# Making the operands of two weight matrices once, beside the attention, and loading their parts later: an encoder layer on one core

## The chip, the core and the metric

The kernel runs on one core of a Trainium2 chip. The metric is the device time of one execution in microseconds (us), the median of several runs. The engines are called PE (TensorE: matmuls, with PEld for its weight loads), DVE (VectorE), ACT (ScalarE), POOL (GpSimd) and SP (SyncE, which here only issues DMAs).

## The reference

One encoder layer in float32 on 2048 tokens of width 1024:

```
proj = x @ w_in                     # queries, keys, values of 16 heads, 8 forget gates
y    = 8 heads of forgetting attention, 8 heads of chunked band attention
x    = layer_norm(alpha * x + concat(y) @ w_out, ln1)       # w_out: 1024 x 1024
u    = causal conv of width 3 over x @ w_up                 # w_up: 1024 x 5632
h    = value * gelu(gate)                                   # halves of u, 2816 wide
out  = layer_norm(alpha * x + h @ w_down, ln2)              # w_down: 2816 x 1024
```

## The kernel before

*Three matmuls for one product.* Each operand of a large product is kept as two float32r parts of 128x512: a high part, a rounded copy that ACT makes (`split`, line 172), and a low part, the source minus the high part, a subtraction on DVE or POOL (line 175). `mm3` (lines 179 to 181) adds up high x high, high x low and low x high in PSUM.

*Seven products for eight.* The up- and down-projections multiply 2 by 2 blocks with seven block products. The table `DOWN` says for each of the seven which block of h, or sum or difference of two, meets which block of w_down, or sum or difference of two, and to which output blocks the product goes. Five of the seven have a sum on the side of h, five on the side of w_down. `combine` makes such an operand: the sum (line 1045), the high part, the low part.

*Stages.* The projection writes queries, keys and values to DRAM, in two halves of 1024 tokens, in steps of three matmuls for each of the 8 slices k of the width; each of the 1024 steps is a `yield`. The attention goes through work items (head pair, head, chunk of 512 tokens). `weave` runs both, a piece of attention and then so many steps of the dense work; where the attention needs heads that are not projected yet, the dense work runs alone (`projected`). The dense work goes on with the output projection of chunks 0 and 1. Then a `Pipeline` runs steps written out in a list: output projection of chunk 2, up-projection of chunks 0 and 1, output projection of chunk 3, down-projection of chunks 0 and 1, up- and down-projection of chunks 2 and 3. A step has `load` (issued up to five steps ahead, as buffers allow), `prepare` (splits and sums, two steps ahead) and `multiply`. Chores (norms, transposes, stores) are taken between steps at a fixed pace. All tiles of 128x512 come from `Slots`, a pool of 54 and later 85 buffers.

*The order within an engine* follows these priorities, as the framework puts the instructions out ahead of time; each engine then works strictly in order. All loads and stores are issued by SP, in one queue.

*Which engine makes a part.* In `out_steps` weights are split by ACT and POOL, tokens by ACT and DVE. In the down-projection h is split by ACT and DVE, w_down by ACT and POOL; sums go to DVE or POOL as `Choice` says, a running account of both engines' work that charges 0.6 for DVE and 1.23 for POOL, lets the account fall by a step's time, and prefers DVE by 3. The down-projection goes through all 11 k of one product before the next (n = 2 and 4 together), in the order 3, 6, 1, 2 and 4, 5, 7, and runs twice, for chunks 0 and 1 and for chunks 2 and 3. So each operand of w_down is made twice, each of w_out four times. One step has 12 matmuls of 512 columns in the down-projection, 24 in the output projection.

Of the kernel before, what the change touches and what calls it, by code (L numbers as in the profile page):

```python
# [19 lines left out]
P = 128  # L20
# [54 lines left out]
    ((3,), ((0, 1), (1, 1)), ((0, 1), (1, 1)), ()),  # L75
    ((6,), ((0, 0),), ((0, 0), (0, 1)), ()),
    ((1,), ((1, 0),), ((0, 0), (1, 1)), ()),
    ((2, 4), (), ((0, 0), (1, 0)), ((1, 0),)),
    ((5,), (), ((1, 1),), ((0, 0),)),
    ((7,), (), ((1, 0), (1, 1)), ((0, 1), (1, 1))),  # L80
)
AHEAD_L, AHEAD_P, RESERVE = 5, 2, 16
# [22 lines left out]
def hymba_layer(  # L105
# [58 lines left out]
    x1t_d = tl(dram, [NCH, KT, P, CH], F32, "x1t_d")  # L164

# [120 lines left out]
    def weave(a, dense, rate):  # L286

        done, start = 0.0, dense.length
        for unit in a:
            done += unit  # L290
            while dense.length - start < done * rate and dense.step():
                pass

# [425 lines left out]
    def out_steps(c, mem, zp, banks, state, done):  # L719
# [4 lines left out]
        def load_tiles(j, ks):  # L724
            for k in ks:
                ws[j, k] = mem.get()
                nc.sync.dma_start(ws[j, k], w_out[k * P : (k + 1) * P, CH * j : CH * j + CH])

        def split_tile(j, k):
            raw = ws[j, k]  # L730
            ws[j, k] = mem.get(F32R), mem.get(F32R)
            split(*ws[j, k], raw, nc.scalar, nc.gpsimd)
            mem.put(raw)

        def product_step(j, t):
# [9 lines left out]
            def prepare():  # L745
                if (j, t) == (0, 0):
                    state["z"] = [{} for _ in range(TQ)]
                    state["stt"] = tl(zp, [P, TQ, 2, 6], F32, "bn", 2)
                    for k, raw in enumerate(ys):
                        split_tile(0, k)  # L750
# [4 lines left out]
            def multiply():  # L755
                acc = banks.get()
                for k in range(KT):
                    mm3(acc, *(y[:, t * P : t * P + P] for y in ys[k]), *ws[j, k], k == 0, k == KT - 1)
                    if t == TQ - 1:
                        mem.put(*ws[j, k])  # L760
                        if j == 0:
                            split_tile(1, k)
# [12 lines left out]
            return Step(load, prepare, multiply, {(0, 0): 32, (0, TQ - 1): WNEXT + 1}.get((j, t), 1), 5.2)  # L775
# [247 lines left out]
    def ffn_down2(ca, mem, zp, banks, gains, later, end):  # L1023
# [63 lines left out]
        def product_step(g, k, n):  # L1087
            ns, blocks, rows, used = DOWN_ORDER[g]
            (i0, j0), u2, aop, (k0, l0), v2, bop, _ = DOWN[n]
            ops = []  # L1090

            def load():
# [5 lines left out]
                if n == ns[0]:  # L1098
                    for i, j in rows:
                        w[g, k, i, j] = mem.get()  # L1100
                        r0 = (HF * i + k) * P
                        nc.sync.dma_start(f32(w[g, k, i, j]), w_down[r0 : r0 + P, CH * j : CH * j + CH])

            def prepare():
                ops.extend(combine(h[i0, j0, k], u2 and h[(*u2, k)], aop, nc.vector))
                ops.extend(combine(w[g, k, k0, l0], v2 and w[(g, k, *v2)], bop, nc.gpsimd))
                if n == ns[-1]:
                    mem.put(*(w.pop((g, k, *b)) for b in rows), *(h.pop((*b, k)) for b in used))
# [34 lines left out]
    with ExitStack() as st:  # L1143
# [42 lines left out]
        def dense_work():  # L1186
            yield from projection(mem, banks, state)
# [26 lines left out]
        with ExitStack() as inner:  # L1214
            projected(1)
# [103 lines left out]
```

## Time and profile before

| | us |
|---|---|
| median of 3 runs | 2919.07 (2910.76 to 2919.12) |
| the profiled execution's own time | 2915.05 |
| its span, from the first to the last instruction | 2913.2 |

| engine | busy us | share of the span | instructions |
|---|---|---|---|
| PE | 2763.0 | 95% | 12632 |
| DVE | 2000.8 | 69% | 3333 |
| ACT | 1247.7 | 43% | 2165 |
| POOL | 1255.8 | 43% | 1178 |

Mean granted clock of TensorE: 0.974 of full speed. DMA moved 399.43 MB, a mean of 137 GB/s.

The table gives means over stages that differ. A busy PE can be a PE that is fed slowly: a stretch is better judged by its number of matmuls than by its busy time. In rows of waits the instruction that waited stands left of the arrow, the one that ended the wait right of it. In rows of groups the line may be that of a helper: line 175 is every low part, whoever asked for it.

### The profile page before, as it was taken

How to read it: one execution, taken by the hardware profiler on the slowest of the kernel's cores; microseconds unless marked ns; L12 is line 12 of the kernel's file. 1: busy time of each engine (PE TensorE's matmuls, PEld its weight loads, DVE VectorE, ACT ScalarE, POOL GpSimd, SP SyncE). 2: the span in 40 equal slices, each digit the busy share in tenths (PEclk: the TensorE clock that was granted, in tenths of full speed). 3: DMA queues.
4: the chain of work that ended last, by engine and by line, in shares of the span. 5: the costliest groups of instructions: out<-in, count | busy, mean ns of one | idle time of the engine just before them, and what ended most of it. 6: DMA issues, size and time to landing. Idle time of an engine off the chain costs nothing.

```text
span 2913.2 us, 38493 instructions
## 1 busy us (share of the span) xinstructions
PE 2763.0 (95%) x12632; PEld 2065.3 (71%) x12632; DVE 2000.8 (69%) x3333; ACT 1247.7 (43%) x2165; POOL 1255.8 (43%) x1178
## 2 busy tenths in 40 slices
PE   8999999999999999998899999998977999999996
PEld 6675767766666667665678888777755888887674
DVE  3446365665454556686877777877798777778878
ACT  3434334344443444444454454533434544454442
POOL 2224331436556654555432211545677211115565
PEclk9999999999999999999999999999988999999998
DMA  6534446443333345646522222577352222228542
GB/s 193 150 120 136 116 154 189 135 139 101 95 106 95 104 139 174 181 154 223 178 84 87 77 83 81 179 239 266 125 166 87 72 84 83 80 76 306 182 141 105
DMA packets 255832, 399.43 MB, mean 137 GB/s; under 512 B 64368, under 2 KB 79856, under 8 KB 255632
## 3 DMA queue, kind: packets, MB, share of 16 engines
q1 hardware_dynamic: 255632, 396.98, 43.1%
q8 instruction: 99, 1.62, 0.2%
q14 instruction: 101, 0.83, 0.1%
HBM read 298.16 MB, written 98.70 MB: 136 GB/s over the span
## 4 chain that ended last, share of the span: by engine, by line
PE 38%; DVE 8%; POOL 3%; DMA 2%; issue 2%; ACT 1%; SPq 0%; POOLq 0%; DVEq 0%; ACTq 0%
PE acc L179 13%; PE acc L180 12%; PE acc L181 12%; DVE slot L175 2%; POOL slot L175 1%; DVE slot L1045 1%; DVE slot L1057 1%; DMA slot<-in_w_down_dram 1%; DVE slot L1075 1%; DVE slot L781 1%; DMA slot<-h_d 1%; ACT slot L172 1%; POOL slot L953 0%; POOL slot L784 0%; DVE slot L870 0%
## 5 line engine op out<-in xcount | busy, mean ns | idle before, releaser
L179 PE MATMUL acc<-slot,slot 128*128 128x512 f32 (+2 forms) x3128 | 1201.7, 384 | 69.0 <-ACT slot L172 31.5
L180 PE MATMUL acc<-slot,slot 128*128 128x512 f32 (+2 forms) x3128 | 1195.0, 382 | 18.6 <-POOL slot L175 18.6
L181 PE MATMUL acc<-slot,slot 128*128 128x512 f32 (+2 forms) x3128 | 1195.0, 382 | 13.9 <-DVE slot L175 12.6
L172 ACT ACTIVATE slot<-slot 128x512 fp32r<-128x512 f32 (+1 forms) x906 | 533.1, 622 | 768.4 <-DVE slot L1045 187.1
L175 POOL TENSOR_TENSOR slot<-slot,slot 128x512 fp32r<-128x512 f32 (+1 forms) x363 | 542.9, 1505 | 512.9 <-ACT slot L172 385.1
L179 PEld LDWEIGHTS acc<-slot,slot 128*128 128x128 f32 x3128 | 602.0, 192 | 196.9 <-ACT slot L172 40.4
L181 PEld LDWEIGHTS acc<-slot,slot 128*128 128x128 f32 x3128 | 600.6, 192 | 138.1 <-DVE slot L175 21.6
L180 PEld LDWEIGHTS acc<-slot,slot 128*128 128x128 f32 x3128 | 602.1, 192 | 135.6 <-POOL slot L175 23.8
L175 DVE TENSOR_TENSOR slot<-slot,slot 128x512 fp32r<-128x512 f32 (+1 forms) x547 | 495.7, 919 | 229.0 <-ACT slot L172 165.7
L598 POOL TENSOR_TENSOR sums<-sums,pt 128x512 f32<-128x512 f32 (+3 forms) x416 | 410.0, 985 | 229.5 <-ACT pt L589 171.3
L589 ACT ACTIVATE pt<-st 128x512 f32<-128x512 f32 (+3 forms) x544 | 262.8, 493 | 390.5 <-PE st L578 140.0
L664 PE MATMUL y<-pt,vv 128*64 128x512 f32 (+3 forms) x1088 | 268.3, 505 | 0.0
L577 PE MATMUL st<-qa,ka 128*128 128x512 f32 (+2 forms) x544 | 210.0, 387 | 8.8 <-ACT pt L589 8.6
L543 DVE TENSOR_REDUCE mx<-sc 128x1 f32<-128x512 f32 x192 | 128.2, 687 | 125.3 <-PE sc L540 123.9
L1045 DVE TENSOR_TENSOR slot<-slot,slot 128x512 f32<-128x512 f32 x180 | 178.6, 1020 | 25.8 <-DMA slot<-in_w_down_dram 9.0
L578 PE MATMUL st<-qb,kb 97*128 97x512 f32 (+2 forms) x544 | 192.0, 359 | 2.8 <-ACT qb L558 2.0
L540 PE MATMUL sc<-kb,qb 66*128 66x512 f32 (+2 forms) x544 | 187.3, 372 | 6.4 <-DMA qb<-qh_d 5.8
L822 DVE SCALAR_TENSOR_TENSOR v<-u,cw,v 128x1024 f32<-128x1024 f32 x88 | 116.4, 1323 | 84.3 <-ACT v L821 84.3
L577 PEld LDWEIGHTS st<-qa,ka 128*128 128x128 f32 x544 | 103.3, 190 | 97.0 <-issue 53.2
L598 POOL TENSOR_TENSOR sums<-pt 128x384 f32<-128x384 f32 (+1 forms) x64 | 77.9, 1216 | 203.3 <-PE sc L616 164.1
L664 PEld LDWEIGHTS y<-pt,vv 128*64 128x64 f32 x1088 | 80.0, 136 | 120.0 <-issue 107.5
L540 PEld LDWEIGHTS sc<-kb,qb 66*128 66x128 f32 x544 | 99.0, 189 | 71.6 <-DVE mx L548 18.1
(108 smaller groups left out, 2172.6 us busy)
## 6 DMA issues: line engine op xcount, KB each, us to landing
slot<-in_w_down_dram SPq DMA_DIRECT2D x242, 256.0 KB
slot<-in_w_up_dram SPq DMA_DIRECT2D x176, 256.0 KB
h_d<-v SPq DMA_DIRECT2D x44, 512.0 KB
slot<-h_d SPq DMA_DIRECT2D x88, 256.0 KB
slot<-in_w_qk_dram SPq DMA_DIRECT2D x66, 256.0 KB
slot<-in_w_out_dram SPq DMA_DIRECT2D x64, 256.0 KB
kb<-kh_d SPq DMA_DIRECT2D x88, 128.0 KB
ka<-kh_d SPq DMA_DIRECT2D x88, 128.0 KB
```

The costliest lines, as they stand in the source:

```text
L172: nc.scalar.activation(hi, src, AF.Copy)
L175: lo_eng.tensor_tensor(lo, src, f32(hi), op=ALU.subtract)
L179: nc.tensor.matmul(acc, wh, mh, start=first, stop=False, **more)
L180: nc.tensor.matmul(acc, wh, ml, start=False, stop=False, **more)
L181: nc.tensor.matmul(acc, wl, mh, start=False, stop=last, **more)
L540: nc.tensor.matmul(sc[:, m0:m1], qb[:KR, tq], kb[:KR, m0:m1], start=True, stop=True)
L577: nc.tensor.matmul(st[:, w2], ka[:, js], qa[:, w2], start=True, stop=False)
L578: nc.tensor.matmul(st[:, w2], kb[:KM, js], qb[:KM, w2], start=False, stop=True)
L589: nc.scalar.activation(pt[:, w], st[:, w], AF.Exp)
L598: nc.gpsimd.tensor_tensor(acc[:, w], (acc if first is None else first)[:, w], pt[:, w], op=ALU.add)
L664: nc.tensor.matmul(y[half, w], v, pt[:, w], start=first and n < 2, stop=last and n >= len(tiles) - 2)
L1045: choice.engine().tensor_tensor(src, f32(u), f32(v), op=op)
```

## The change

A generator `prepare_weights` is stepped by the projection, once every ninth step from step 63 on. It loads the raw tiles of w_out and w_down, makes the two parts of each of the 16 tiles of w_out, and of each of the 77 operands of the down-projection (with its sum where it has one), on ACT and DVE, and stores both parts in DRAM (`wo_d`, `wd_d`). It has four raw buffers and one buffer for a pair of parts. The output projection and the down-projection no longer split or add weights: their `load` fetches the two parts into two slots. What a `Pipeline` step asks for in slots changes with it. After the projection what is left of the generator is run out.

```diff
@@ -72,13 +72,15 @@
 }
 
 DOWN_ORDER = (
-    ((3,), ((0, 1), (1, 1)), ((0, 1), (1, 1)), ()),
-    ((6,), ((0, 0),), ((0, 0), (0, 1)), ()),
-    ((1,), ((1, 0),), ((0, 0), (1, 1)), ()),
-    ((2, 4), (), ((0, 0), (1, 0)), ((1, 0),)),
-    ((5,), (), ((1, 1),), ((0, 0),)),
-    ((7,), (), ((1, 0), (1, 1)), ((0, 1), (1, 1))),
+    ((3,), ((0, 1), (1, 1)), ()),
+    ((6,), ((0, 0),), ()),
+    ((1,), ((1, 0),), ()),
+    ((2, 4), (), ((1, 0),)),
+    ((5,), (), ((0, 0),)),
+    ((7,), (), ((0, 1), (1, 1))),
 )
+
+PRE0, PRE = 60, 9
 AHEAD_L, AHEAD_P, RESERVE = 5, 2, 16
 DLY_V, DLY_R, DLY_Z = 32, 16, 16
 WNEXT = 3
@@ -163,6 +165,9 @@
     h_d = tl(dram, [NF, P, S], F32, "h_d")
     x1t_d = tl(dram, [NCH, KT, P, CH], F32, "x1t_d")
 
+    wo_d = tl(dram, [KT, 2, 2, P, CH], F32, "wo_d")
+    wd_d = tl(dram, [NF // 2, 8, 2, P, CH], F32, "wd_d")
+
     halo = tl(consts, [P, 2, NF, 2], F32, "halo")
     cw = tl(consts, [P, 2, NF, 4], F32, "cw")
 
@@ -290,6 +295,42 @@
             done += unit
             while dense.length - start < done * rate and dense.step():
                 pass
+
+    def prepare_weights(pool):
+
+
+
+        def parts(dst, u, v=None, op=None):
+            hl = tl(pool, [P, 2, CH], F32R, "w_hl")
+            if v is not None:
+                src = f32(hl[:, 1])
+                nc.vector.tensor_tensor(src, u, v, op=op)
+                u = src
+            split(hl[:, 0], hl[:, 1], u, nc.scalar, nc.vector)
+            nc.sync.dma_start(dst.rearrange("l p m -> p l m"), f32(hl))
+
+        def load(src, tiles):
+            raws = []
+            for n, (i, j) in enumerate(tiles):
+                raws.append(tl(pool, [P, CH], F32, f"w_raw{n}"))
+                nc.sync.dma_start(raws[n], src[i * P : i * P + P, CH * j : CH * j + CH])
+            return raws
+
+        for k in range(0, KT, 2):
+            tiles = [(k + n // 2, n % 2) for n in range(4)]
+            raws = load(w_out, tiles)
+            yield
+            for raw, (i, j) in zip(raws, tiles):
+                yield
+                parts(wo_d[i, j], raw)
+        HF = NF // 2
+        for k in range(HF):
+            raws = load(w_down, [(HF * i + k, j) for i in range(2) for j in range(2)])
+            yield
+            for n in DOWN:
+                yield
+                (k0, l0), v, op = DOWN[n][3:6]
+                parts(wd_d[k, n], raws[2 * k0 + l0], v and raws[2 * v[0] + v[1]], op)
 
 
     def projection(mem, banks, state):
@@ -723,14 +764,9 @@
 
         def load_tiles(j, ks):
             for k in ks:
-                ws[j, k] = mem.get()
-                nc.sync.dma_start(ws[j, k], w_out[k * P : (k + 1) * P, CH * j : CH * j + CH])
-
-        def split_tile(j, k):
-            raw = ws[j, k]
-            ws[j, k] = mem.get(F32R), mem.get(F32R)
-            split(*ws[j, k], raw, nc.scalar, nc.gpsimd)
-            mem.put(raw)
+                ws[j, k] = mem.get(F32R), mem.get(F32R)
+                for n in range(2):
+                    nc.sync.dma_start(f32(ws[j, k][n]), wo_d[k, j, n])
 
         def product_step(j, t):
             def load():
@@ -747,7 +783,6 @@
                     state["z"] = [{} for _ in range(TQ)]
                     state["stt"] = tl(zp, [P, TQ, 2, 6], F32, "bn", 2)
                     for k, raw in enumerate(ys):
-                        split_tile(0, k)
                         ys[k] = mem.get(F32R), mem.get(F32R)
                         split(*ys[k], raw, nc.scalar, nc.vector)
                         mem.put(raw)
@@ -759,7 +794,6 @@
                     if t == TQ - 1:
                         mem.put(*ws[j, k])
                         if j == 0:
-                            split_tile(1, k)
                             load_tiles(1, range(k + WNEXT, min(k + WNEXT + 1, KT)))
                         else:
                             mem.put(*ys[k])
@@ -772,7 +806,7 @@
                 if (j, t) == (1, TQ - 1):
                     done()
 
-            return Step(load, prepare, multiply, {(0, 0): 32, (0, TQ - 1): WNEXT + 1}.get((j, t), 1), 5.2)
+            return Step(load, prepare, multiply, {(0, 0): 40, (0, TQ - 1): 2 * WNEXT + 1}.get((j, t), 1), 5.2)
 
         return [product_step(j, t) for j in range(2) for t in range(TQ)]
 
@@ -1085,8 +1119,8 @@
         held = []
 
         def product_step(g, k, n):
-            ns, blocks, rows, used = DOWN_ORDER[g]
-            (i0, j0), u2, aop, (k0, l0), v2, bop, _ = DOWN[n]
+            ns, blocks, used = DOWN_ORDER[g]
+            (i0, j0), u2, aop = DOWN[n][:3]
             ops = []
 
             def load():
@@ -1095,17 +1129,15 @@
                         h[i, j, k] = mem.get()
                         cs = slice((ca + i) * CH, (ca + i + 1) * CH)
                         nc.sync.dma_start(f32(h[i, j, k]), h_d[HF * j + k, :, cs])
-                if n == ns[0]:
-                    for i, j in rows:
-                        w[g, k, i, j] = mem.get()
-                        r0 = (HF * i + k) * P
-                        nc.sync.dma_start(f32(w[g, k, i, j]), w_down[r0 : r0 + P, CH * j : CH * j + CH])
+                w[n, k] = mem.get(F32R), mem.get(F32R)
+                for l in range(2):
+                    nc.sync.dma_start(f32(w[n, k][l]), wd_d[k, n, l])
 
             def prepare():
                 ops.extend(combine(h[i0, j0, k], u2 and h[(*u2, k)], aop, nc.vector))
-                ops.extend(combine(w[g, k, k0, l0], v2 and w[(g, k, *v2)], bop, nc.gpsimd))
+                ops.extend(w.pop((n, k)))
                 if n == ns[-1]:
-                    mem.put(*(w.pop((g, k, *b)) for b in rows), *(h.pop((*b, k)) for b in used))
+                    mem.put(*(h.pop((*b, k)) for b in used))
 
             def multiply():
                 if k == 0:
@@ -1184,7 +1216,11 @@
             return done
 
         def dense_work():
-            yield from projection(mem, banks, state)
+            for n, t in enumerate(projection(mem, banks, state)):
+                yield t
+                if n >= PRE0 and n % PRE == 0:
+                    next(state["weights"], None)
+            run_all(state["weights"])
             for n in range(4):
                 gains.append(mem.get())
                 src = ln1[n // 2, n % 2 * CH : n % 2 * CH + CH]
@@ -1212,6 +1248,7 @@
                 dense.step()
 
         with ExitStack() as inner:
+            state["weights"] = prepare_weights(inner.enter_context(tc.tile_pool(name="w_s", bufs=1, side="right")))
             projected(1)
             pools = attention_pools(inner)
             weave(attention(pools, [0, 1], lambda p: projected(p // 2 + 1)), dense, RATE1)
```

## Rows read from the trace of the kernel before

**Rows 1.** Stretches: length, busy us (instructions) of each engine, granted clock, DMA share, GB/s.

```profile
53.00:1170.00 1117.00, 1097.67 (x5591) 762.11 (x5590) 609.89 (x1545) 444.38 (x880) 492.03 (x519) 0.99 0.43 131
1362.00:1378.00 16.00, 8.85 (x27) 4.05 (x25) 16.00 (x17) 8.99 (x16) 13.27 (x9) 0.96 0.40 139
1500.00:1850.00 350.00, 350.00 (x1513) 283.64 (x1512) 266.46 (x308) 174.11 (x251) 67.51 (x108) 1.00 0.26 82
1922.50:2100.00 177.50, 162.93 (x693) 130.26 (x691) 132.87 (x154) 71.59 (x122) 103.10 (x68) 0.95 0.62 211
2100.00:2250.00 150.00, 113.48 (x393) 85.77 (x394) 142.26 (x158) 59.96 (x102) 103.64 (x65) 0.84 0.37 120
...
2750.00:2913.20 163.20, 131.96 (x528) 103.08 (x527) 135.04 (x172) 56.57 (x97) 105.90 (x65) 0.91 0.36 121
2675.00:2700.00 25.00, 25.00 (x110) 20.29 (x109) 22.11 (x25) 8.53 (x14) 14.60 (x10) 1.00 0.94 342
```

**Rows 2.** Waits of PE, 1922.5 to 2100 us: us in total, times, longest.

```profile
PE acc L179 <- ACT slot L810: 5.0, 1, 5.0
PE acc L807 <- DVE slot L781: 4.8, 4, 1.3
```

**Rows 3.** Waits of PE, 2654 us to the end.

```profile
PE acc L180 <- POOL slot L175: 12.0, 5, 9.5
```

**Rows 4.** Chain that ended last, 2100 to 2260 us: start us, us, what.

```profile
by line: DVE slot L175 21.7%; issue 12.7%; DVE slot L1045 9.5%; DVE slot L1057 7.5%; DVE slot L1075 6.5%; POOL slot L784 6.2%; POOL slot L175 5.5%; POOL slot L953 5.1%; DVE slot L870 4.4%; DMA slot<-in_w_up_dram 4.2%; DVE bn L1066 3.1%; PE 
...
2220.72 1.30 POOL slot L953
...
2248.85 3.49 DMA slot<-in_w_up_dram
```

**Rows 5.** The same chain, 2780 us to the end.

```profile
2858.41 5.51 DMA slot<-in_w_down_dram
...
2870.25 9.96 POOL slot L175
```

**Rows 6.** Groups by line and shape, 1362 to 1378 us: busy, mean ns, idle.

```profile
L175 POOL TENSOR_TENSOR slot<-slot,slot 128x512 fp32r<-128x512 f32 x8 | 13.6, 1729 | 0.0
L175 DVE TENSOR_TENSOR slot<-slot,slot 128x512 fp32r<-128x512 f32 x7 | 10.8, 1580 | 0.0
```

**Rows 7.** Groups on DVE, 1500 to 1850 us.

```profile
L953 DVE TENSOR_TENSOR slot<-slot,slot 128x512 f32<-128x512 f32 x72 | 49.4, 686 | 4.9 <-PE acc L180 2.8
```

**Rows 8.** Groups on DVE, 2100 to 2250 us.

```profile
L175 DVE TENSOR_TENSOR slot<-slot,slot 128x512 fp32r<-128x512 f32 x48 | 52.3, 1120 | 3.1 <-ACT slot L172 3.1
L1075 DVE SCALAR_TENSOR_TENSOR slot<-slot,mv,slot 128x512 f32<-128x512 f32 x16 | 20.6, 1310 | 0.0
L1045 DVE TENSOR_TENSOR slot<-slot,slot 128x512 f32<-128x512 f32 x18 | 18.9, 1080 | 0.0
```

**Rows 9.** Groups on POOL, 2100 to 2250 us.

```profile
L175 POOL TENSOR_TENSOR slot<-slot,slot 128x512 fp32r<-128x512 f32 x31 | 48.2, 1566 | 31.1 <-ACT slot L172 28.6 <-DMA slot<-in_w_down_dram 2.5
```

**Rows 10.** Groups on DVE and POOL, 2750 us to the end.

```profile
L175 DVE TENSOR_TENSOR slot<-slot,slot 128x512 fp32r<-128x512 f32 x44 | 43.6, 1012 | 19.6 <-ACT slot L172 13.1 <-POOL slot L175 6.4
...
L175 POOL TENSOR_TENSOR slot<-slot,slot 128x512 fp32r<-128x512 f32 x43 | 73.4, 1721 | 31.2 <-ACT slot L172 31.0
```

**Rows 11.** Groups on DVE, 53 to 1170 us.

```profile
L175 DVE TENSOR_TENSOR slot<-slot,slot 128x512 fp32r<-128x512 f32 x80 | 63.4, 801 | 60.5 <-DMA v_d<-slot 31.0 <-ACT slot L172 21.4 <-DMA kh_d<-slot 3.8
```

**Rows 12.** Groups on ACT, 53 to 1170 us.

```profile
L172 ACT ACTIVATE slot<-slot 128x512 fp32r<-128x512 f32 x110 | 68.2, 629 | 60.4 <-DMA slot<-in_w_qk_dram 26.2 <-DMA slot<-in_xT_dram 7.6 <-PE acc L181 6.4
```

**Rows 13.** Waits of PE, 53 to 1170 us.

```profile
PE sc L540 <- DMA qb<-qh_d: 4.8, 7, 1.2
PE acc L179 <- ACT slot L172: 3.9, 1, 3.9
```

**Rows 14.** One stretch in which only values are projected.

```profile
316.00:335.00 19.00, 19.00 (x163) 18.97 (x161) 0.69 (x1) 3.74 (x9) 0.46 (x1) 1.00 0.34 89
```

**Rows 15.** Line 1102, issues on SP: min/median/max ns, first and last start.

```profile
L1102 SPq DMA_DIRECT2D slot<-in_w_down_dram x242: 327/374/705, 1868.7 to 2866.3; - x121
```

## Prediction

> **What bounds the kernel now.** I first cut the span into stretches, one row of busy times each [rows 1]. From 1500 to 1850 us, the middle of the first up-projection, PE is busy all the time and passes 1513 matmuls in 350 us: 0.2313 us for one of 512 columns. That is the yardstick: a stretch that takes longer than its matmuls times 0.2313 is not set by PE. The reader should hold each row against it:
> - 53 to 1170 (projection woven with attention): PE busy 1097.67 of 1117, idle 19.3 us. PE sets the time; DVE is busy 55%, ACT 40%, POOL 44%.
> - 1362 to 1378 (output projection of chunk 2): 27 matmuls, 6 us of work in 16: 10 lost.
> - 1922.5 to 2100 (down-projection of the first two chunks): 693, of them 32 short transposes (some 5 us): 661 x 0.2313 + 5 = 158; 19 lost.
> - 2100 to 2250 (its end and the start of the next up-projection): 393 give 91 of 150: 59 lost, granted clock 0.84.
> - 2750 to the end: 528 give 122 of 163: 41 lost, clock 0.91; both are mixes of 2.4 and 1.2 GHz.
>
> So some 130 us are lost in the places where the changed operands are made today. Then I asked who PE waits for. In the early down-projection it is the norm's copy and the norm itself on DVE [rows 2]; in the last one POOL's low parts, 12.0 us, the longest wait 9.5 [rows 3]. The chain of 2100 to 2260 lies on DVE, and towards the end on POOL (norm L784, up-weight sums L953); at the tail it goes through 9.96 us of POOL low parts [rows 4, 5]. DVE, not PE, is the full engine there: 142 of 150 us.
>
> Why DVE is full: between 1362 and 1378, with POOL and DVE both subtracting, a DVE instruction of 128x512 takes 1.580 us and POOL's 1.729 [rows 6]; the same kind takes DVE 0.686 in the up-projection, where POOL has little to do [rows 7]. POOL's low parts cost DVE's time also.
>
> **The change, part by part.** The span, 2913.2 us, lies in an execution of 2915.05 us, and the sum is made against that; the median of the three runs is 4.0 above it.
>
> *Removed.* For each of the 64 output-weight tiles and of the 2 x 77 down-projection operands: one ACT high part and one POOL low part; and for 2 x 55 operands a sum, mostly on DVE. In later stages that is 218 ACT and 218 POOL instructions. PE's matmuls stay the same in number.
>
> (a) Output projection. From 1362 on PE is fed one k at a time at POOL's 1.7 us [rows 6]. With the weights' low parts gone DVE's 0.686 is left for the tokens'. I take back 8 of 10; for chunks 0 and 1, which run inside the attention, and chunk 3 I count nothing.
>
> (b) 1922.5 to 2100. The waits for the norm's copy and norm, 5.0 and 4.8 [rows 2], stand behind a DVE stretched by POOL; the granted clock of 0.95 costs 0.05 x 178 = 9. I take half of both, 10 of 19.
>
> (c) 2100 to 2250. DVE's stretching: 48 x (1.120 - 0.686) + 18 x (1.080 - 0.686) + 16 x (1.310 - 0.686) = 20.8 + 7.1 + 10.0 = 37.9 us, against 103.6 us of POOL work [rows 1, 8]: 0.37 us for each us of POOL. Of POOL go some 20 of the 31 low parts (two groups of eleven operands end here) and some 4 sums, 24 x 1.566 = 37 us [rows 9]: 14 us for DVE, and some 7 sums of its own, 5 us. That is 18 us of the DVE-led part. The POOL-led part (in the chain from 2220.7 to the load at 2248.9, [rows 4]) has 37 us less queued in front of it; it is shortened by at most its 28, I take 15. Next late is DVE with token splits and norm, which stay. Together 33 of 59.
>
> (d) 2750 to the end. POOL's 43 low parts of 73.4 us [rows 10] are nearly all weights'. The 12.0 us of PE's waits on them go [rows 3]. DVE's 44 splits are stretched by 44 x (1.012 - 0.686) = 14 [rows 10], its other instructions likewise; 14 more for that and for its sums. Together 26 of 41; the last norm stays.
>
> Sum of the gains: 8 + 10 + 33 + 26 = 77.
>
> *Added, beside the attention.* From projection step 63 on (about 53 us), every ninth step, one of 93 parts: 16 output tiles and 77 down operands. That is 93 ACT, 93 + 55 = 148 DVE instructions. The nearest row of that stretch: 80 splits on DVE at 0.801, 110 on ACT at 0.629 [rows 11, 12]. So 148 x 0.801 = 119 us on DVE (55 to 65%) and 58 on ACT (40 to 45%), under PE's 1098. What covers it is PE's work; without that cover it would be 119. The same kind of split is in the stretch already, and PE's waits show 3.9 us for it, once, and 4.8 for queries behind SP [rows 13]. Values are projected in bursts: the 19 us from 316 hold 163 matmuls, six times the 27 of nine steps, so a part in 3.2 us; there DVE is busy 0.69 of 19 [rows 14], so the work itself fits. SP gets 60 raw loads and 93 stores of 512 KB, 0.374 each to issue [rows 15]: 57 us over 1117. A store waits for its low part, and behind it on SP stand the loads of queries and keys. The parts have one buffer: each waits for the store before it. A 256 KB load lands after 3.49 to 5.51 us [rows 4, 5]; for a store of twice that I take 5 (bounds 3.5 and 11), a cycle of 0.80 + 0.63 + 0.80 + 0.37 + 5 = 7.6 against 1117/107 = 10.4 us from part to part on average. So it keeps up, except in the bursts. Bounds: nothing, or 119. I take 12: the trace's own splits are far nearer the lower end; 5 for bursts, 5 for a doubled wait for queries, 2 for the clock.
>
> The Trainium skill ("DMA: Bandwidth & Descriptors", Anatomy of one DMA) gives 2.0 us plus bytes over 436e3 for a transfer on the GpSimd path: 3.2 us for such a store, an estimate, by which the 5 would be 3.2; no row here times a store of that size, and the rows' 3.49 and 5.51 for half of it lie above that.
>
> *Moved to loads.* The down-projection loads 308 tiles of 256 KB in place of 242, the output projection 128 in place of 64. The first three groups (n = 3, 6, 1) load as many as before, two for each operand. The 66 more come with n = 2, 4 (four in place of two per k) and 5 (two in place of one): 768 KB or less in 12 x 0.2313 = 2.78 us, 283 GB/s. A stretch with PE full moved 342 [rows 1]. The output projection's 64 more spread over four chunks, whose first step now asks for 40 slots and not 32 before it starts. I count nothing for either; exposed, 66 x 0.262 MB / 342 GB/s = 50, and 49 for the 64.
>
> Against the hope in (a) to (d) speaks a rule of the Trainium skill ("GPSIMD Engine Reference", Specifications): GpSimd shares its SBUF interfaces with VectorE, contended when the DVE instruction has two SBUF inputs. It holds beside the attention as well, where POOL adds up probabilities 44% of the time: at the both-busy price of rows 6 the 148 would be 148 x 1.58 = 234 us. The row there says 0.801, and still under PE.
>
> Sum: 2915 - 77 + 12 = 2850; set against the median, **2854**.
>
> **The rivals.**
> 1. *The attention pays (slower).* The single buffer: once a store takes over 10.4 - 2.6 = 7.8 us, ACT and DVE, both in order, stand at the next part's first write while exponentials, maxima and evictions queue behind, and PE waits for them. For it: the bound of 11 us, the bursts of 3.2. Against: DVE at 55%, and few waits of PE in rows 13. It turns the sign from 77/93 = 0.83 us a part. Wholly exposed: 2919 - 77 + 119 = 2961.
> 2. *DVE stays the bound.* In (c) and (d) norms, adds and token splits fill DVE anyway, and only what PE waits for by name on POOL goes: 12.0, with 8 in (a) and 10 for the rest: 30. For it: most of that chain's time by line is DVE's [rows 4]. 2919 - 30 + 12 = 2901.
> 3. *Loads.* Half of the 130 extra are exposed, because a step's weights arrive after its tokens: 2919 - 77 + 12 + 50 = 2904. Against: 342 GB/s under a full PE.
>
> **How the numbers follow.** My forecast 0.70, rival 1 0.09, rival 2 0.15, rival 3 0.06. The low end: of the 130 lost all but some 25 (last norm, transposes) come back at no cost, 2919 - 105 = 2814. The high end reaches rival 2: 2902. Measurement tells 0.3% from no change, about 9 us: faster by more 0.86 (forecast, and most of rivals 2 and 3), within it 0.05, slower 0.09 (rival 1).
>
> **What would show it.** (a) the first step of chunk 2 takes 6 to 8 us, not 16; (c) DVE's L175 falls under 0.9 us and the stretch after n = 7 loses under 30 us; (d) no POOL low part at the tail. Attention: the projection's last matmul comes at most 12 to 15 us later. Wrong if the projection ends 60 us later with PE waiting for ACT or DVE, or if PE in the down-projections waits for loads of parts.

## The result, and the profile after

The changed kernel takes 2848.98 us, the median of 4 runs (2845.75 to 2853.64), against 2918.18 (2910.76 to 2919.12) of the kernel before in the same session: ratio 0.977, 95% interval 0.9748 to 0.9791. The forecast was 2854, in a range of 2814 to 2902. The profiled execution took 2845.75 us, its span is 2843.8, and TensorE's mean granted clock rose from 0.974 to 0.99. POOL's busy time fell from 1255.8 to 897.4 us, and DMA moved 498.01 MB in place of 399.43.

To find where the 69.4 us of span came from, I cut both traces where each stage's first matmul starts. At the cut before "output, chunk 2" PE has started 6608 instructions in both kernels, so the first row compares the same work: projection, attention, and output projection of chunks 0 and 1.

| stage | before, us | after, us | difference |
|---|---|---|---|
| all up to output, chunk 2 | 1362.0 | 1385.5 | +23.5 |
| output, chunk 2 | 61.2 | 53.6 | -7.6 |
| up, chunks 0 and 1 | 454.7 | 456.8 | +2.1 |
| output, chunk 3 | 44.6 | 44.4 | -0.2 |
| down, chunks 0 and 1 | 275.4 | 229.9 | -45.5 |
| up, chunks 2 and 3 | 456.2 | 448.8 | -7.4 |
| down, chunks 2 and 3 | 250.7 | 216.5 | -34.2 |
| the last norm | 8.4 | 8.2 | -0.2 |

The first row holds three things. The projection's last matmul starts 22.2 us later than before (1192.7 us against 1170.5). After it, up to the last eight matmuls before the cut, 3.6 us come back. Then PE waits 4.8 us for chunk 2's own first operands. SP issues the eight loads of chunk 2's tokens behind the sixteen loads of its parts (of which these are the last six), and ACT has the first of them 6.1 us after that issue began (rows of one view, 1375.9 to 1387 us):

```profile
1375.97 2.69 SPq L769 DMA_DIRECT2D slot<-wo_d  x6
1378.71 5.43 SPq L777 DMA_DIRECT2D slot<-y_d  x8
...
1384.85 1.35 ACT L177 ACTIVATE slot<-slot 128x512 fp32r<-128x512 f32 x2 [2.12 <-DMA slot<-y_d]
...
1385.53 0.80 PE L184 MATMUL acc<-slot,slot 128*128 128x512 f32 x1 [4.83 <-ACT slot L177]
```

So of the 23.5 us 18.6 come from the attention and what follows it (22.2 less 3.6), and 4.9 from the loading of chunk 2.

The changed kernel moves the lines: splits stand at L177 (ACT) and L180 (DVE, POOL), the three matmuls at L184 to L186, sums at L1079, the norm at L1109, L815 and L818. The parts' sum is L307, their store L310.

Stretches of the changed kernel, in the columns of [rows 1]:

```profile
53.00:1185.00 1132.00, 1100.02 (x5552) 757.95 (x5551) 717.36 (x1680) 486.02 (x955) 499.99 (x512) 0.99 0.60 183
1385.50:1439.20 53.70, 51.19 (x225) 40.11 (x226) 34.20 (x47) 18.49 (x34) 10.52 (x7) 0.97 0.77 273
1940.40:2117.90 177.50, 176.21 (x776) 142.11 (x775) 100.67 (x153) 43.88 (x72) 17.52 (x12) 1.00 0.82 277
2117.90:2260.00 142.10, 122.01 (x488) 94.44 (x487) 134.15 (x151) 64.73 (x104) 79.30 (x53) 0.94 0.39 124
2675.00:2843.80 168.80, 158.92 (x683) 127.57 (x682) 112.12 (x172) 40.47 (x66) 31.19 (x21) 0.99 0.62 202
```

Read the third line against the fourth of [rows 1]: the same stage, the same 177.50 us, 776 matmuls in place of 693. POOL is busy 17.5 us and not 103.1, and DVE 100.7 and not 132.9. Those 83 matmuls at 0.2313 are 19.2 us. The fourth line answers to 2100 to 2250: 488 matmuls at 0.2313 are 112.9, so some 29 us are lost and not 59; DVE is still the fullest engine, 134 of 142 us. The last line: 683 give 158.0 of 168.8, 11 lost and not 41.

PE's waits there, from 1940 to 2118 us, answering to [rows 2], and then from 2619 us to the end, answering to [rows 3]:

```profile
PE acc L184 <- DVE slot L1091: 0.7, 3, 0.2
PE acc L184 <- ACT slot L177: 0.6, 1, 0.6
```

```profile
PE acc L186 <- DVE slot L180: 1.3, 3, 0.6
PE acc L184 <- ACT slot L177: 0.4, 1, 0.4
```

The waits for norm and POOL are gone, and in these two stretches no wait for a loaded part has come in their place. DVE's groups from 2118 to 2260 us, and POOL's, answering to [rows 8, 9]:

```profile
L180 DVE TENSOR_TENSOR slot<-slot,slot 128x512 fp32r<-128x512 f32 x53 | 50.2, 972 | 3.5 <-ACT slot L177 3.3
L1109 DVE SCALAR_TENSOR_TENSOR slot<-slot,mv,slot 128x512 f32<-128x512 f32 x15 | 21.6, 1467 | 0.0
```

```profile
L180 POOL TENSOR_TENSOR slot<-slot,slot 128x512 fp32r<-128x512 f32 x19 | 30.9, 1633 | 25.5 <-ACT slot L177 25.5
L818 POOL TENSOR_TENSOR slot<-slot,slot 128x512 f32<-128x512 f32 x8 | 14.9, 1879 | 7.0 <-ACT slot L817 7.0
```

POOL still makes 19 low parts here, those of the next up-projection, and DVE's norm is even slower than before (1.467 against 1.310). In the last down-projection POOL has no low part left, and DVE's L180 takes this from 2680 us on, where [rows 10] had 1012:

```profile
L180 DVE TENSOR_TENSOR slot<-slot,slot 128x512 fp32r<-128x512 f32 x50 | 36.0, 736 | 34.8 <-ACT slot L177 28.2 <-PE acc L185 6.5
```

The other side of the account is the attention, 53 to 1185 us. PE's waits, answering to [rows 13]:

```profile
PE st L618 <- ACT pt L630: 7.2, 9, 2.7
PE acc L184 <- ACT slot L177: 7.1, 2, 6.9
PE sc L581 <- DMA qb<-qh_d: 4.8, 6, 1.2
PE sc L581 <- DVE mx L589: 3.2, 2, 1.8
PE st L619 <- ACT qb L599: 2.9, 4, 1.5
```

All PE waits of this stretch with a named releaser come to 31 us, against 20.8 before: many small ones, exponentials and queries that come late. The longest, 6.9 us for ACT, ends at 80.8 us, where the kernel before waited 3.9. DMA's share rose from 0.43 to 0.60. And DVE and ACT do stand at the parts' one buffer until its store has landed; DVE waits for raw tiles too (waits of DVE, then of ACT):

```profile
DVE w_hl L307 <- DMA wd_d<-w_hl: 18.0, 13, 3.7
...
DVE w_hl L307 <- DMA w_raw<-in_w_down_dram: 11.8, 3, 5.9
```

```profile
ACT w_hl L177 <- DMA wo_d<-w_hl: 9.1, 5, 3.5
ACT w_hl L177 <- DMA wd_d<-w_hl: 6.2, 8, 1.4
```

### The profile page after: what moved, and what is told of

The parts are those of the page before. It is cut to its first block, busy times and chain, and to the rows that moved or that the text cites. A ratio compares the mean times of both kernels' runs of the same rounds, so it can differ in the third digit from the quotient of the medians.

```text
span 2843.8 us, 38496 instructions
## 1 busy us (share of the span) xinstructions
PE 2740.9 (96%) x12632; PEld 2046.2 (72%) x12632; DVE 1933.6 (68%) x3391; ACT 1175.7 (41%) x2036; POOL 897.4 (32%) x940
## 2 busy tenths in 40 slices
DMA packets 308487, 498.01 MB, mean 175 GB/s; under 512 B 68896, under 2 KB 84384, under 8 KB 308288
## 4 chain that ended last, share of the span: by engine, by line
PE 64%; DVE 6%; issue 3%; DMA 3%; POOL 2%; ACT 1%; SPq 0%; POOLq 0%; DVEq 0%; ACTq 0%
PE acc L184 17%; PE acc L186 17%; PE acc L185 17%; PE y L705 5%; PE sc L581 3%; PE st L618 3%; PE st L619 2%; DVE slot L180 2%; DMA qb<-qh_d 1%; DVE slot L1109 1%; PE sc L657 1%; DMA slot<-y_d 1%; DVE slot L815 1%; ACT slot L177 0%; PE acc L841 0%
## 5 line engine op out<-in xcount | busy, mean ns | idle before, releaser
L184 PE MATMUL acc<-slot,slot 128*128 128x512 f32 (+2 forms) x3128 | 1189.6, 380 | 46.3 <-ACT slot L177 30.2
L186 PE MATMUL acc<-slot,slot 128*128 128x512 f32 (+2 forms) x3128 | 1184.5, 379 | 12.2 <-DVE slot L180 10.6
L184 PEld LDWEIGHTS acc<-slot,slot 128*128 128x128 f32 x3128 | 594.2, 190 | 171.6 <-ACT slot L177 35.8
L177 ACT ACTIVATE slot<-slot 128x512 fp32r<-128x512 f32 (+1 forms) x688 | 410.3, 622 | 730.0 <-DVE slot L1079 143.2
L186 PEld LDWEIGHTS acc<-slot,slot 128*128 128x128 f32 x3128 | 592.8, 190 | 138.5 <-DVE slot L180 20.0
L185 PEld LDWEIGHTS acc<-slot,slot 128*128 128x128 f32 x3128 | 594.0, 190 | 113.4 <-issue 3.2
L180 DVE TENSOR_TENSOR slot<-slot,slot 128x512 fp32r<-128x512 f32 (+1 forms) x548 | 448.2, 828 | 255.4 <-ACT slot L177 227.1
L639 POOL TENSOR_TENSOR sums<-sums,pt 128x512 f32<-128x512 f32 (+3 forms) x416 | 421.2, 1012 | 237.8 <-ACT pt L630 182.7
L180 POOL TENSOR_TENSOR slot<-slot,slot 128x512 fp32r<-128x512 f32 (+1 forms) x144 | 197.6, 1374 | 304.1 <-ACT slot L177 249.0
L705 PE MATMUL y<-pt,vv 128*64 128x512 f32 (+3 forms) x1088 | 280.3, 505 | 0.2 <-DVE yt L647 0.2
L589 DVE CUSTOM_DVE_ANT_0 junk<-sc,bq 128x512 bf16<-128x512 f32 (+2 forms) x224 | 108.3, 483 | 47.8 <-PE sc L581 39.0
```

The lines of the kernel that those rows point to most:

```text
L177: nc.scalar.activation(hi, src, AF.Copy)
L180: lo_eng.tensor_tensor(lo, src, f32(hi), op=ALU.subtract)
L184: nc.tensor.matmul(acc, wh, mh, start=first, stop=False, **more)
L185: nc.tensor.matmul(acc, wh, ml, start=False, stop=False, **more)
L186: nc.tensor.matmul(acc, wl, mh, start=False, stop=last, **more)
L639: nc.gpsimd.tensor_tensor(acc[:, w], (acc if first is None else first)[:, w], pt[:, w], op=ALU.add)
```

## The experiments

Theory: the down-projections get 80 us back because POOL's work there, and the sums, no longer slow and fill DVE, and their loads are hidden; the attention hides the parts' making but for a small price. Rivals: the loads of parts are exposed; DVE stays the bound; the price is the one buffer's hold. Ratios are against the kernel before. The "price of the attention" is the start of output chunk 2 less 1362.0 us, 23.5 in the changed kernel. It moves by some 5 us without any edit there: two runs below that change only the down-projection (e5, e6) show 23.1 and 28.9. It is read from one profiled execution of each kernel, and has chunk 2's wait of some 5 us in it. Expectations below that speak of 15 to 18 us were written with that price as read earlier on the way: the first matmul of the output projection comes 14.8 us late, the eighth-last before the cut 18.6.

### Does POOL's work slow the down-projections?

**e7.** The kernel before, with the low parts of its down weights on DVE:

```diff
-  ops.extend(combine(w[g, k, k0, l0], v2 and w[(g, k, *v2)], bop, nc.gpsimd))
+  ops.extend(combine(w[g, k, k0, l0], v2 and w[(g, k, *v2)], bop, nc.vector))
```

> The kernel before with one argument changed: the low parts of the down-projection's weights are made by DVE, not POOL. Nothing is made beforehand. If the stretching is the loss, DVE's own 154 x 0.69 us are less than what it gets back, and this alone gains: 2880 to 2900. If DVE's load was the bound whoever else works, it is no faster than before or slower: 2915 to 2950.

Measured 2891.57 us, ratio 0.9915 (0.99 to 0.9931): 25 us faster than before (0.0085 of 2918), though DVE does more. That is the first reading. The first down-projection takes 261.4 us, the second 239.7. DVE's groups from 1922 to 2110 us:

```profile
L175 DVE TENSOR_TENSOR slot<-slot,slot 128x512 fp32r<-128x512 f32 x120 | 84.7, 737 | 21.0 <-ACT slot L172 15.7 <-PE acc L180 4.2 <-issue 0.4
L1045 DVE TENSOR_TENSOR slot<-slot,slot 128x512 f32<-128x512 f32 x66 | 46.9, 733 | 6.5 <-DMA slot<-h_d 3.5 <-PE acc L181 1.4 <-DMA slot<-in_w_down_dram 0.8
```

With POOL busy for only 34 of these 188 us a DVE instruction is at 0.73 to 0.74. A third or so of what the whole change wins could be had by one argument.

**e5 and e6.** The changed kernel with one subtraction more in each of the 154 steps of the down-projections, whose result nobody reads; on POOL in e5, on DVE in e6:

```diff
                 ops.extend(w.pop((n, k)))
+                nc.gpsimd.tensor_tensor(idle[0], f32(ops[0]), f32(ops[0]), op=ALU.subtract)
```

> The changed kernel with one POOL subtraction of 128x512 in each of the 154 steps of the down-projections, on h's high part, its result read by nobody: POOL works beside DVE as before the change, but PE waits for none of it. If DVE's stretching by POOL was the loss, most of (b) and (c) and half of (d) comes back, 35 to 50 us: 2885 to 2900, with DVE's low parts and sums in the down-projection near 0.95 us again. If PE and the queues waited for the weights' parts themselves, the time stays within 8 us of 2849.

> The same 154 idle subtractions on DVE in place of POOL: 154 x 0.69 = 106 us of DVE work in the down-projections, no work on POOL. DVE was busy 57% in the steady part there, so that part should hold it; only the stretch after the last product, where DVE is full, pays for its 22 to 30 of them: 15 to 20 us, 2865 to 2870. If it pays less than 8, DVE isn't the bound of that stretch any more.

Measured: e5 2878.84 us, ratio 0.9865 (0.984 to 0.989), so 30 us of the gain are given back; e6 2875.41, 0.9861 (0.9844 to 0.9877), 26 given back; e5 is 6 us under its expected range, e6 5 us over. The stages part them. In e5 the two down-projections take 249.8 and 228.7 us, 32 more, spread over both. DVE's groups of e5 from 2118 to 2270 us, and POOL's:

```profile
L180 DVE TENSOR_TENSOR slot<-slot,slot 128x512 fp32r<-128x512 f32 x52 | 57.5, 1132 | 5.3 <-ACT slot L177 5.3
```

```profile
L1139 POOL TENSOR_TENSOR idle<-slot 128x512 f32<-128x512 f32 x15 | 20.9, 1395 | 18.6 <-ACT slot L177 18.1
```

Work on POOL whose result nobody reads brings DVE's split from 0.972 back to 1.132, where it was before the change (1.120, [rows 8]). The second down-projection shows it for one and the same set of instructions, first in the changed kernel (from 2619 us), then in e5 (2640 to 2870 us):

```profile
L180 DVE TENSOR_TENSOR slot<-slot,slot 128x512 fp32r<-128x512 f32 x71 | 50.5, 723 | 53.2 <-ACT slot L177 44.3 <-PE acc L185 8.6
...
L1079 DVE TENSOR_TENSOR slot<-slot,slot 128x512 f32<-128x512 f32 x41 | 27.6, 686 | 17.3 <-PE acc L186 9.1 <-PE acc L185 4.3 <-DMA slot<-h_d 3.9
```

```profile
L180 DVE TENSOR_TENSOR slot<-slot,slot 128x512 fp32r<-128x512 f32 x71 | 65.9, 944 | 43.4 <-ACT slot L177 40.8 <-PE acc L185 1.5 <-issue 0.8
L1079 DVE TENSOR_TENSOR slot<-slot,slot 128x512 f32<-128x512 f32 x41 | 45.3, 1118 | 9.5 <-PE acc L186 3.4 <-DMA slot<-h_d 3.3 <-PE acc L185 2.7
```

The 30 us are not the stretching alone, though. The idle subtractions also stand in POOL's order before the sums that POOL still makes: from 2640 to 2870 us ACT waits 22.4 us for those sums in e5, and 15.7 in the changed kernel. No run parts the two.

In e6 the down-projections take 243.8 and 220.1 us, 17.5 more, and 11.7 of those lie in the last 11 steps of the first one, 52.5 us for 40.8 (in the changed kernel the groups of 11 steps before it take 30.4 to 33.9, in e6 30.4 to 34.0). There DVE is full, 91.87 of 92 us from 2118 to 2210; elsewhere in the down-projections it has room, but for 2 us more in the first and 4 in the second. Of the rest of e6's loss 4.8 us lie in the last norm (13.0 us for 8.2), and 5 in the attention, within the scatter named above.

The Trainium skill ("GPSIMD Engine Reference", Specifications) has GpSimd share its SBUF interfaces with VectorE, contended for DVE instructions with two SBUF inputs; the trace agrees: 0.73 beside a quiet POOL, 1.13 beside a busy one. The prediction set this rule against (a) to (d); it is what they rest on.

### What is the output projection's half worth?

**e8.** The changed kernel without parts of w_out; the output projection splits its weights itself, as before:

```diff
-        for k in range(0, KT, 2):
-            tiles = [(k + n // 2, n % 2) for n in range(4)]
-            raws = load(w_out, tiles)
...
+                    for k, raw in enumerate(ys):
+                        split_tile(0, k)
```

> Only the down-projection's operands are made beforehand; the output projection splits its weights itself, on ACT and POOL, as before. By the prediction's terms the output part is worth 8 us and its 16 parts cost 16/93 of the attention's price, some 3: 2854 us. The rival reading, that what chunk 2 gained is paid back at the start of the up-projection because the norms there set the time, gives 2847 to 2850.

Measured 2855.37 us, ratio 0.9786 (0.9771 to 0.9802). Chunk 2 is at 61.3 us again, as before. The 16 output parts so bring some 6 us, as the prediction's terms had it; the two intervals still overlap. Their absence does not lower the price of the attention (24.6), though PE no longer waits before chunk 2: its first matmul starts 0.2 us after the one before.

### What does the attention pay for?

**e2.** Each part's sum, high part and low part made twice, stored once:

```diff
+            for _ in range(2):
+                src = u
...
+                split(hl[:, 0], hl[:, 1], src, nc.scalar, nc.vector)
```

> Each part's sum, high and low part are computed twice, one after the other, into the same buffer; loads and stores are as in the changed kernel. If the 15 to 18 us that the attention pays is the price of DVE and ACT instructions in the queues of these engines, twice the work pays about twice: some 2864 us in all, the first output-projection matmul near 1208 us. If it is the price of transfers that arrive later, the time stays within 5 us of the changed kernel's 2849.

Measured 2886.64 us, ratio 0.9891 (0.9875 to 0.9907): 38 above the changed kernel, price of the attention 61.8: neither reading, the second making costs more than the first. The largest of PE's waits from 53 to 1185 us is for the exponentials; that they are late because the doubled work stands before them in ACT's and DVE's order is my reading:

```profile
PE st L619 <- ACT pt L631: 17.2, 16, 3.1
```

**e3.** Each pair of parts stored twice, the second time to another place (49 MB more, and the buffer held until both have landed):

```diff
             nc.sync.dma_start(dst.rearrange("l p m -> p l m"), f32(hl))
+            nc.sync.dma_start(wx_d[next(extra)].rearrange("l p m -> p l m"), f32(hl))
```

> Each pair of parts is stored twice, the second time to a place that nobody reads: 49 MB more beside the attention, no more computing. If transfers are the attention's price (a load of value weights came late and held ACT, behind it the row that PE waited for), the price goes up by half or more: 2857 to 2868 us, first output-projection matmul at 1200 us or later. If it is DVE and ACT work, 2849 to 2852.

Measured 2943.57 us, ratio 1.0082 (1.0064 to 1.01): slower than before. The price of the attention is 118.4. I had expected 20 us at most.

**e11.** To part the transfers from the buffer's hold: behind each store a copy of 512 KB from DRAM to DRAM, which holds no buffer (49 MB written and 49 read):

```diff
+            e = next(extra)
+            nc.sync.dma_start(wx_d[e], w_down[e % 10 * 2 * P : (e % 10 + 1) * 2 * P, :CH])
```

> The changed kernel with a copy of 512 KB from DRAM to DRAM behind each store of a pair of parts: as many more bytes written as when the pair was stored twice, which cost 95 us, but the buffer of parts isn't held by it. If the one buffer, held longer, was what cost (ACT and DVE standing at the next part's first write), this stays under 2870. If it was the DMA queues, it costs about as much as storing twice, 2920 or more.

Measured 2929.33 us, ratio 1.0042 (1.0028 to 1.0057), price 106.0. The stretch of 53 to 1185 us in e3, and then in e11, against the first line of the changed kernel's:

```profile
53.00:1185.00 1132.00, 1067.08 (x5066) 708.57 (x5066) 670.92 (x1505) 452.77 (x885) 465.09 (x469) 0.96 0.66 208
```

```profile
53.00:1185.00 1132.00, 1054.25 (x5065) 712.47 (x5064) 669.68 (x1516) 455.98 (x890) 465.20 (x469) 0.96 0.70 214
```

Every engine is less busy than in the changed kernel, and DMA's mean share is only 0.66 and 0.70. The granted clock is 0.96 in both where the changed kernel has 0.99: 0.03 of 1132 us, so some 34 us of each loss are TensorE's clock, by this estimate, and come on top of the waits. Nearly half of e3's price arises from 505 to 720 us, where it grows from 37 to 89 us, at a clock of 0.90 (0.10 of 215 us is 21):

```profile
505.00:720.00 215.00, 181.81 (x819) 121.30 (x817) 132.36 (x331) 80.55 (x163) 48.42 (x71) 0.90 0.72 224
```

What comes late stands in PE's waits, of e3 and of e11:

```profile
PE st L622 <- DMA qa<-qh_d: 13.0, 2, 10.2
PE st L622 <- ACT pt L634: 10.8, 14, 1.7
PE acc L185 <- ACT slot L178: 9.9, 5, 5.7
```

```profile
PE st L623 <- ACT pt L635: 18.3, 14, 4.7
PE sc L586 <- DMA qb<-qh_d: 15.2, 10, 4.8
PE st L624 <- ACT qb L604: 11.5, 9, 2.5
```

Queries are late, and what ACT and DVE do behind them. In e11 DVE and ACT also stood 66 us for the stores (27.6, 20.9 and 17.7) against 33, probably because a store lands later with a copy behind it in the queue. So the copy did not take the hold out altogether: 93 more transfers which hold no buffer themselves turn the sign, but how much of that goes by way of the longer hold is not shown.

**e14.** The parts' stores issued by POOL and not SP, so that SP's loads no longer stand behind them:

```diff
-            nc.sync.dma_start(dst.rearrange("l p m -> p l m"), f32(hl))
+            nc.gpsimd.dma_start(dst.rearrange("l p m -> p l m"), f32(hl))
```

> The stores of the parts are issued by POOL in place of SP, and so go through another DMA queue; nothing else changes. If the attention's own loads come late because they stand behind the parts' stores in SP's queue, the 18 us that the attention pays fall by half: 2838 to 2843 us. If it is the DMA engines' time that is short, whatever the queue, 2846 to 2852. If POOL, now waiting for low parts, delays the sums that the attention divides by, slower than 2855.

Measured 2923.39 us, ratio 1.002 (1.0004 to 1.0036), price 97.4. POOL's waits from 53 to 1185 us, and the stores that it issues (duration min/median/max in ns):

```profile
POOL wd_d L310 <- DVE w_hl L180: 129.6, 30, 8.6
...
POOL wo_d L310 <- DVE w_hl L180: 28.9, 5, 7.0
```

```profile
L310 POOL DMA_DIRECT2D wd_d<-w_hl x77: 725/727/737, 161.2 to 963.1; - x77
```

This is the third reading. POOL waits for DVE's low part before it can issue, and the sums of the probabilities stand behind. The buffer is held longer too: DVE alone waits 52.4 us for these stores. So the run does not tell what SP's queue alone costs. For such DMAs the trace records the landing: 3.15 us after the issue at the least, 4.14 in the median, 7.19 at most. The Trainium skill ("DMA: Bandwidth & Descriptors", Anatomy of one DMA) gives a formula for this path, by which 512 KB take 3.2 us, an estimate: the least agrees, under this load the median is 0.9 longer. For the stores that SP issues, which the prediction put at 5 us, the trace gives no such times.

**e9.** The parts' low halves on POOL:

```diff
-            split(hl[:, 0], hl[:, 1], u, nc.scalar, nc.vector)
+            split(hl[:, 0], hl[:, 1], u, nc.scalar, nc.gpsimd)
```

> The low parts that are made beside the attention are made by POOL, not DVE: 93 instructions less on DVE there, and POOL goes from 44 to some 55% busy. By the price of computing twice (38 us for 148 DVE and 93 ACT instructions) the 93 are worth up to 10 to 15 us if DVE's queue is what pays: 2835 to 2840. Since POOL stretches DVE, and its sums end late in each head, the rival is no gain: 2848 to 2860.

Measured 2865.44 us, ratio 0.9825 (0.9809 to 0.9842), price 39.9, though DVE has 93 instructions less: slower than either reading. PE waits 17.9 us, 13 times, for exponentials (7.2 in the changed kernel), and DVE and ACT wait 75 us for the stores of a buffer that is released later.

**e4 and e15.** The parts spread over the dense work's time and not over its count of steps, every 4.4 us of it in e4; in e15 every 5.0, on into the output projection of chunks 0 and 1:

```diff
+                due += t if n >= PRE0 else 0.0
-                if n >= PRE0 and n % PRE == 0:
+                if due >= 4.4:
+                    due -= 4.4
                     next(state["weights"], None)
```

> A part is made after each 4.4 of projected work as the kernel counts it (0.65 for a step of queries and keys, 0.33 for one of values) instead of after nine steps, so the bursts of one part in 3.2 us go. If the bursts with the single buffer cost the 5 us that I put down for them, about 2844 us and fewer waits of DVE and ACT for the parts' stores than the 36 us of the changed kernel; if they cost nothing, 2849.

> The parts are spread evenly over the projected work and on over the output projection of chunks 0 and 1, one part in each 5.0 of dense work as the kernel counts it, until the attention ends near 1380 us. Spreading evenly alone gave 2843. If the price is transfers that collide, thinner traffic takes another 3 to 6 us off: 2837 to 2840. If the output projections, which load parts themselves in that time, collide with the stores now, 2843 to 2850.

Measured: e4 2842.96 us, ratio 0.9745 (0.9729 to 0.976), price 18.2; e15 2850.67, 0.9771 (0.9755 to 0.9787), price 29.1. e4 comes as its first reading has it in time, but the waits for the stores stay at 32 us (33 in the changed kernel), so what was won is not these waits. e15 is at the edge of its second reading.

**e16.** e4 with two buffers for a part; the room comes from the attention's tiles `row` (2 to 1) and `yt` (3 to 2):

```diff
-            hl = tl(pool, [P, 2, CH], F32R, "w_hl")
+            hl = tl(pool, [P, 2, CH], F32R, "w_hl", 2)
```

> The kernel after with the parts spaced evenly over the dense work (as e4, 2843) and with two buffers instead of one for a part's halves; the room comes from one buffer less of the row tile and of the norm's output tile. If the one buffer's hold is part of the attention's price: the waits of DVE and ACT for the parts' stores fall from 32 to under 10 us, the first output matmul comes some 4 to 8 us earlier than the 1188 us of e4, and the time is 2835 to 2840. If the price is the transfers' alone: the waits for stores fall as well, but the first output matmul stays at 1185 to 1190 and the time at 2841 to 2846. If the fewer row and norm buffers hold up the attention's ends: over 2850, with waits on those tiles.

Measured 2842.80 us (5 runs), ratio 0.9745 (0.9732 to 0.9758), price 23.0. The first output matmul comes at 1191.6 us (1188.1 in e4). DVE's waits for the stores and, at the same first write of a part, for loads, and then ACT's for the stores:

```profile
DVE w_hl L307 <- DMA wd_d<-w_hl: 9.6, 10, 2.0
DVE w_hl L307 <- DMA w_raw<-in_w_down_dram: 9.4, 2, 7.0
DVE w_hl L307 <- DMA vv<-v_d: 7.4, 1, 7.4
```

```profile
ACT w_hl L177 <- DMA wd_d<-w_hl: 3.6, 3, 2.4
...
ACT w_hl L177 <- DMA wo_d<-w_hl: 1.6, 2, 1.0
```

The waits for the stores halved, 32 to 15 us, and nothing came of it in the time. But DVE does not stand less at a part's first write: there it now waits for loads, 27 us in all where e4 has 21. So the run does not show that the hold is slack; it shows that a second buffer by itself gains nothing here. The smaller `row` and `yt` may hide a gain of a few us; no run parts that, and none has more raw buffers.

e4 and e16 are the best versions measured. Their intervals meet that of the changed kernel at the edge, so the 6 us between them are likely, not sure.

## Why the prediction was right

Direction, size and mechanism came as forecast, 2849 for 2854. But both sides of the sum were too small, and that the errors cancelled is luck: gains of 94.7 us (7.6 + 45.5 + 7.4 + 34.2) where I had 77, and a price of 23.5 where I had 12, with 2 more in the first up-projection. Counted by PE's instructions, the stretches of (b), (c) and (d) gain 22.0, 30.1 and 30.1 us.

- **(a)** 8 taken, 7.6 measured; but the 4.8 us that PE waits before chunk 2 stand against it, so some 3 are left there. e8 gives 6 for the half as a whole. The sign to watch was off: chunk 2's first 24 matmuls take 11.2 us, not 6 to 8. DVE's low parts did not fall to 0.686, beside a POOL that still adds in the norm of the chunk before; from 1385.5 to 1397 us:

```profile
L180 DVE TENSOR_TENSOR slot<-slot,slot 128x512 fp32r<-128x512 f32 x8 | 9.5, 1227 | 0.8 <-ACT slot L177 0.8
```

```profile
L818 POOL TENSOR_TENSOR slot<-slot,slot 128x512 f32<-128x512 f32 x4 | 6.6, 1672 | 24.1 <-ACT slot L817 23.8 <-DMA slot<-wo_d 0.3
```

- **(b)** Undersized: I took half of 19; PE's rate shows that all 19 came back. The step that failed is the halving: with POOL at 17.5 us of 177.5 PE's waits for the norm and its copy are gone, and the clock is at 1.00.
- **(c)** 33 taken, some 30 measured (59 lost, now 29). Its working has a slip of 1 us: 14 and 5 are 19, not 18. DVE's L180 stayed at 0.972 and did not fall under 0.9, because POOL goes on with the up-projection's weights, 79 us busy in that stretch. What left DVE there is the weights' sums (18 sums in [rows 8], 8 now) more than the stretching. How much the shorter queue on POOL brought, for which I took 15, was not measured by itself.
- **(d)** 26 taken, 30.1 measured for the same stretch; from 2675 us on 11 us are left as lost. The stage as a whole gains 34.2: 4.3 come before 2750 us, where the sum had nothing.
- **The mechanism** is shown from both sides: POOL's low parts moved away alone win 25 (e7), idle work put back on POOL loses 30 (e5). By e5 the stretching of DVE is up to 30 of the 87 us won around the down-projections; that the rest is the removed instructions and sums was not tried by itself.
- **Loads** cost nothing in the down-projections, as taken: the second down-projection passes its groups of 11 steps in 30.5 to 32.5 us at a DMA share of 0.80 (2630 to 2810 us), where 30.5 is the matmuls' own time (11 x 12 x 0.2313). There rival 3 fell. In the output projection nothing was the wrong size: the 4.8 us before chunk 2 are tokens that come behind twice as many loads of weights.
- **DVE as the bound** (rival 2) holds in one place above all, the last group of the first down-projection with the norm and the up-projection's start: 40.8 us for 30.5 of matmuls, and e6 adds 11.7 just there.
- **The attention** (rival 1) was much nearer than the 0.09 that I gave, and the sign that I named was missed: the projection's last matmul came 22.2 us later, not 12 to 15 at most. The sum had 12: 5 for bursts, 5 for queries, 2 for the clock. Of these the queries' wait did not double (4.8 in both), the clock did not fall, and what came instead is exponentials, 7.2 in 9 waits, and ACT's split, 7.1. Whether my reason, the single buffer, sets the price is open: a second buffer changed nothing in the time, but DVE then waited for loads at the same place (e16). Doubling the work costs 38 (e2), adding 49 MB stored costs 95 (e3); each of the two is more than the whole 23.5, so the price is not proportional to either, and some 34 us of e3's loss are the clock. At today's rate most of both is hidden, and there is little cover left. How the 18.6 before chunk 2's wait divide between transfers, the buffer and the engines' order stays open, as does whether e3's loss arises in SP's order of issue or in the transfers themselves.

## What to carry to other kernels

A tile split on GpSimd is paid for twice where VectorE is the bound: look at what one and the same VectorE instruction takes in a stretch with GpSimd quiet and in one with it busy, and count the difference over all of VectorE's work there. Where one load becomes two, look at what SP issues behind them: the load that is late may be another one. Work that is moved under a stage that another engine fills can be nearly free at one rate and, at twice the transfers, decide the sign; so before adding more, double the added work and, separately, the added transfers, and see how near the edge is. When a forecast comes true, compare stage by stage all the same: here two wrong terms cancelled.

## What was not expected of the hardware

With DMA's mean share at 0.66 to 0.70 and no engine but PE near full, 93 more transfers of 512 KB in 1.1 ms cost 80 to 95 us (e3, e11), some 34 of them by TensorE's clock as estimated above: a mean share well under one does not say that loads arrive in time. In e3 the issues themselves got longer: SP's `DMA_DIRECT2D` took over 1 us 62 times in 53 to 1185 us, against 20 times in the changed kernel. A store issued by POOL costs it 0.727 us, one issued by SP 0.377 in the median.
